# Hybrid decoder trunk: the second weight pair on ScalarE's queue, the first weight cast on VectorE, nine warming products

## The chip, the cores and the metric

The kernel runs on one core of one Trainium2 chip. The metric is the device time of one execution in microseconds. Three executions of the kernel before are shown, and a fourth was profiled.

## The reference, cut to what matters

The layer is a decoder block over 272 tokens (16 meta tokens and 256 others) of width 2048. It normalises the tokens, multiplies them by one wide input projection, runs eight retention heads and four mLSTM heads on slices of the product, projects back, and applies a gated MLP with a causal convolution.

```python
u = rmsnorm(h, norm_mix)
proj = u @ w_in.astype(u.dtype)
q_r, k_r, v_r, g_r, q_m, k_m, v_m, o_m, i_pre, f_pre = jnp.split(proj, IN_OFFSETS, axis=-1)
...
mix = jnp.concatenate([ret, hm], axis=-1).astype(h.dtype) @ w_out.astype(h.dtype)
h = h + mix
u = rmsnorm(h, norm_ffn)
up = causal_dwconv(u @ w_up.astype(u.dtype), ffn_conv_w, ffn_conv_b)
gate, val = jnp.split(up, [FFN_DIM], axis=-1)
return h + (jax.nn.silu(gate) * val) @ w_down.astype(h.dtype)
```

## The kernel before, in words

Every product runs on TensorE in float32r with both operands split into a high and a low part. For an operand pair (w, x) three matmuls are made: high by high, high by low, low by high. The high part of a weight (`whi`) is a cast of the loaded tile (`wraw`), and the low part (`wlo`) is `wraw` minus `whi`. The same holds for the activations: `xh` is the cast of the token matrix `hT` times the gain of the norm (ScalarE, L219), and `xl` is the rest (VectorE, L220).

The change touches the first stage alone, the loop at L207. It walks over 16 blocks of 128 rows of the inner dimension (k = 0 to 15): the first two blocks singly, then seven pairs (2,3), (4,5) to (14,15). For each step it loads the tokens `hT` (L209), in the first step also the 16 columns of `par` that hold the gain (L211), and the weights `wraw` from `in_w` (L215). The weights of one block are 320 columns wide: 256 columns of two projections (tiles `k_ps` and `q_ps`) and 64 of the gates. Then it makes `xh` and `xl` per block, `whi` (L224), `wlo` (L226) and the gates' low part (L227). Eight matmuls of a block follow: three for `k_ps` and three for `q_ps` (L136, L137, L139), and two for the gates (L235, L236).

SyncE's queue (SPq) issues nearly all transfers. The weights of blocks 0 and 1 are issued by ScalarE's queue (ACTq). `wraw` has four buffers, so the load of the fifth step waits until the first buffer is read. Ahead of the loop TensorE runs `WARM` products of a constant tile (L199), whose result is not used; one such product shows as two matmul records in the trace.

The order of the instructions on each engine is not the order of the program's text: a scheduler with a simulated time line chooses it when the kernel is built, unless a line asks for an order with `tc.issue_after`. In the text the activations (L219) stand ahead of the cast of the weights (L224).

Of the kernel before, what the change touches and what calls it, by code (L numbers as in the profile page):

```python
# [31 lines left out]
HALF = KT // 2  # L32
GW = 64
W0 = GW + 2 * P
WARM = 8

# [45 lines left out]
def trunk(ctx: ExitStack, tc: tile.TileContext, io, out: bass.AP):  # L84
    nc = tc.nc

    def pool(name, bufs, **kw):
        return tc.tile_pool(name=name, bufs=bufs, **kw)
# [12 lines left out]
    def pcol(name, i, n=1):  # L101
        a = _COLS[name][0]
        return par[:, a + i : a + i + n]
# [28 lines left out]
    def mmk(ps, w, ks, xh, xl, first, last):  # L132

        hi, lo = w
        for k, kk in ks:
            nc.tensor.matmul(ps, hi[:, k, :], xh(kk), start=kk == first, stop=False)  # L136
            nc.tensor.matmul(ps, hi[:, k, :], xl(kk), start=False, stop=False)  # L137
        for k, kk in ks:
            nc.tensor.matmul(ps, lo[:, k, :], xh(kk), start=False, stop=kk == last)  # L139
# [6 lines left out]
    def project(src, xh, xl, t0, ps=None):  # L146

        if ps is None:
            ps = mm.tile([P, 512], F32, name="mmps")
        for half in range(2):  # L150
            half_tile(ps[:, : xh.shape[2] - t0], src, half, xh, xl, t0)
        return ps
# [6 lines left out]
    def rsqrt_m2(work, v, n, after):  # L159

        r0 = work.tile([P, T], F32, name="r0", bufs=1)
        with tc.issue_after(table("natural_log_exp_and_others", after).ins):
            nc.scalar.activation(r0[:, :n], v, AF.Ln, bias=epsc)
        nc.scalar.activation(r0[:, :n], r0[:, :n], AF.Exp, scale=-0.5)
        t = work.tile([P, T], F32, name="rt", bufs=1)
        nc.scalar.activation(t[:, :n], r0[:, :n], AF.Square)
        nc.vector.scalar_tensor_tensor(out=t[:, :n], in0=v, scalar=EPS, in1=t[:, :n], op0=ALU.add, op1=ALU.mult)
        nc.vector.scalar_tensor_tensor(out=r0[:, :n], in0=t[:, :n], scalar=3.0, in1=r0[:, :n], op0=ALU.subtract, op1=ALU.mult)
        return r0
# [27 lines left out]
    warm = at.tile([P, 512], F32, name="atps")  # L197
    for _ in range(WARM):
        nc.tensor.matmul(warm[:, :P], ones, ones, start=True, stop=True)  # L199
# [6 lines left out]
    with pool("sq", 1, side="right") as sqp:  # L206
        for k0, k1 in [(0, 1), (1, 2)] + [(k, k + 2) for k in range(2, KT, 2)]:  # L207
            n = k1 - k0
            nc.sync.dma_start(hT[:, k0:k1, :], io["xT"][:, k0:k1, :])  # L209
            if k0 == 0:  # L210
                nc.sync.dma_start(par[:, 0:KT], io["par"][:, 0:KT])  # L211
            raw = wpool.tile([P, 2, W0], F32, name="wraw", bufs=4)[:, :n, :]

            queue = nc.scalar if k0 < 2 else nc.sync
            load = queue.dma_start(raw, io["w0"][:, k0:k1, :])  # L215
            if k0 >= 2:
                last_load = load
            for k in range(k0, k1):
                nc.scalar.activation(xh[:, k, :], hT[:, k, :], AF.Copy, scale=pcol("gmix", k))  # L219
                nc.vector.scalar_tensor_tensor(out=xl[:, k, :], in0=hT[:, k, :], scalar=pcol("gmix", k),  # L220
                                               in1=xh[:, k, :].bitcast(F32), op0=ALU.mult, op1=ALU.subtract)

            hi = wpool.tile([P, 2, W0 + GW], F32R, name="whi", bufs=5)[:, :n, :]
            copied = nc.scalar.copy(hi[:, :, 0:W0], raw)  # L224
            lo = wpool.tile([P, 2, 2 * P], F32R, name="wlo", bufs=5)[:, :n, :]
            nc.vector.tensor_tensor(out=lo, in0=raw[:, :, 0 : 2 * P], in1=hi[:, :, 0 : 2 * P].bitcast(F32), op=ALU.subtract)  # L226
            parted = nc.vector.tensor_tensor(out=hi[:, :, W0:], in0=raw[:, :, 2 * P :], in1=hi[:, :, 2 * P : W0].bitcast(F32), op=ALU.subtract)  # L227
            for k in range(k0, k1):
                i = k - k0
                first, last = k == 0, k == KT - 1  # L230
                for j, (ps, t0) in enumerate(((k_ps, 0), (q_ps, TQ))):
                    w = hi[:, :, j * P : (j + 1) * P], lo[:, :, j * P : (j + 1) * P]
                    mmk(ps[:, : T - t0], w, [(i, k)], lambda k: xh[:, k, t0:], lambda k: xl[:, k, t0:], 0, KT - 1)
                if not last:
                    nc.tensor.matmul(gates_ps[:, :T], hi[:, i, 2 * P :], xh[:, k, :], start=first, stop=False)  # L235
                nc.tensor.matmul(gates_ps[0:GW, :T], hi[:, i, 2 * P : W0], xl[:, k, :], start=False, stop=False)  # L236
                if last:
                    nc.tensor.matmul(gates_ps[:, :T], hi[:, i, 2 * P :], xh[:, k, :], start=False, stop=True)
        with tc.issue_after(last_load.ins):
            nc.sync.dma_start(par[:, KT:NPAR0], io["par"][:, KT:NPAR0])  # L240

        v0_ps = project(next(tiles), xh, xl, 0, at.tile([P, 512], F32, name="atps"))

        sum4 = None
        for k in range(0, KT, 4):

            sq = rope if k % 8 else sqp.tile([P, 4, T], F32, name="sq" if k else "sum4")
            with tc.issue_after(copied.ins):
                squared = nc.scalar.activation(sq, hT[:, k : k + 4, :], AF.Square)
            if k:  # L250
                with tc.issue_after(parted.ins), tc.high_priority():
                    nc.vector.tensor_tensor(out=sum4, in0=sum4, in1=sq, op=ALU.add)
            else:
                sum4 = sq
        with tc.high_priority():
            for n in (2, 1):
                nc.vector.tensor_tensor(out=sum4[:, 0:n, :], in0=sum4[:, 0:n, :], in1=sum4[:, n : 2 * n, :], op=ALU.add)
            ms = at.tile([P, 512], F32, name="atps")
            nc.tensor.matmul(ms[:, :T], inv_dm, sum4[:, 0, :], start=True, stop=True)
            r = rsqrt_m2(wk, ms[:, :T], T, squared)  # L260
            nc.vector.tensor_scalar(out=rstd1, in0=r[:, :T], scalar1=-0.5, scalar2=None, op0=ALU.mult)
# [39 lines left out]
    for i, x in enumerate((rM, rm)):  # L301
        hi, lo = parts[0:MH, i, :], parts[GW // 2 : GW // 2 + MH, i, :]
# [332 lines left out]
    for half in range(2):  # L635
        mh = midp.tile([P, NHF, SEQ], F32R, name="mh")
        ml = midp.tile([P, NHF, SEQ], F32R, name="ml")
        for jj in range(NHF):
# [10 lines left out]
            copied = nc.scalar.copy(mh[:, jj, :], gt)  # L649
# [147 lines left out]
```

## Time and the profile before

| | |
|---|---|
| median of three runs | 1236.26 us (1235.96 to 1236.76) |
| the profiled execution | 1236.06 us |
| its span, first to last instruction | 1234.3 us |
| outside the span | 1.76 us |
| granted TensorE clock, mean | 0.998 |

The profiled execution is 0.20 us under the median and inside the range of the three runs. The span runs from the first to the last instruction; the time of an execution has 1.76 us beside it.

### The profile page before, as it was taken

The page shows a single profiled execution, that of the slowest core. Times are in us where ns is not written, and L with a number is a line of the kernel's source. Part 1 is how long each engine was busy: PE and PEld are TensorE (multiplying, and loading weights), DVE is VectorE, ACT ScalarE, POOL GpSimd, SP SyncE. Part 2 cuts the span into 40 slices and gives each one's busy share as a digit, 9 for nine tenths or more (in the row PEclk, how much of TensorE's full clock was granted, in tenths as well). Part 3 has the DMA queues.
Part 4 walks back from the last instruction along what each step waited for, and adds up shares of the span by engine and source line. Part 5 has one row for each costly group of instructions (what it writes and reads, how often), then busy time and mean ns, then how long its engine had stood idle before and what let it go on. Part 6 is the DMA issues. An engine that isn't in the chain of part 4 may idle for free.

```text
span 1234.3 us, 22246 instructions
## 1 busy us (share of the span) xinstructions
PE 1223.8 (99%) x9082; PEld 1173.4 (95%) x9082; DVE 831.9 (67%) x1227; ACT 654.9 (53%) x879; POOL 63.0 (5%) x71
## 2 busy tenths in 40 slices
PE   9999999999999999999999999999999999999997
PEld 9999999999999999999999998889999999998886
DVE  8957777756665766778878764445677677664452
ACT  8756656555556556555555543334555555554441
POOL 0100011111110110000000000000000000000000
PEclk9999999999999999999999999999999999999999
DMA  8755454555553656555555655665555555555661
GB/s 276 265 172 164 151 164 160 170 169 163 175 178 121 221 177 217 185 177 186 186 176 187 187 179 187 189 189 186 185 184 181 182 185 184 179 185 187 187 205 69
DMA packets 63687, 224.30 MB, mean 182 GB/s; under 512 B 7392, under 2 KB 8544, under 8 KB 63456
## 3 DMA queue, kind: packets, MB, share of 16 engines
q1 hardware_dynamic: 62352, 219.26, 56.2%
q0 software_dynamic: 656, 2.76, 0.7%
q8 instruction: 71, 1.16, 0.4%
q10 hardware_dynamic: 576, 0.85, 0.2%
q14 instruction: 32, 0.26, 0.1%
HBM read 220.75 MB, written 2.10 MB: 181 GB/s over the span
## 4 chain that ended last, share of the span: by engine, by line
PE 98%; ACT 0%; DMA 0%; DVE 0%; issue 0%; SPq 0%; DVEq 0%; ACTq 0%
PE mmps L137 25%; PE mmps L136 25%; PE mmps L139 25%; PE atps L664 7%; PE atps L665 7%; PE atps L668 7%; PE atps L353 1%; PE atps L345 0%; PE atps L330 0%; DMA wraw<-in_w 0%; PE atps L136 0%; PE atps L139 0%; PE atps L354 0%; PE atps L137 0%; PE atps L346 0%; PE atps L355 0%
## 5 line engine op out<-in xcount | busy, mean ns | idle before, releaser
L127 ACT CAST whi<-wraw 128x1024 fp32r<-128x1024 f32 x404 | 422.9, 1049 | 473.5 <-PE mmps L137 256.8
L129 DVE TENSOR_TENSOR wlo<-wraw,whi 128x1024 fp32r<-128x1024 f32 x404 | 494.7, 1226 | 192.9 <-ACT whi L127 188.0
L137 PE MATMUL mmps<-ul,whi 128*128 128x258 f32 x1408 | 345.8, 283 | 0.0
L136 PE MATMUL mmps<-uh,whi 128*128 128x258 f32 x1408 | 345.5, 282 | 0.0
L136 PEld LDWEIGHTS mmps<-uh,whi 128*128 128x128 f32 x1408 | 266.1, 189 | 0.1
L137 PEld LDWEIGHTS mmps<-ul,whi 128*128 128x128 f32 x1408 | 265.1, 188 | 0.1
L137 PE MATMUL mmps<-xl,whi 128*128 128x272 f32 (+2 forms) x864 | 219.3, 287 | 0.0
L136 PE MATMUL mmps<-xh,whi 128*128 128x272 f32 (+2 forms) x864 | 219.2, 287 | 0.0
L139 PE MATMUL mmps<-uh,wlo 128*128 128x258 f32 x1408 | 198.9, 284 | 0.0
L139 PEld LDWEIGHTS mmps<-uh,wlo 128*128 128x128 f32 x1408 | 182.4, 189 | 0.0
L137 PEld LDWEIGHTS mmps<-xl,whi 128*128 128x128 f32 x864 | 162.9, 189 | 0.0
L136 PEld LDWEIGHTS mmps<-xh,whi 128*128 128x128 f32 x864 | 162.6, 188 | 0.0
L664 PE MATMUL atps<-whi,mh 128*128 128x512 f32 (+1 forms) x360 | 140.5, 391 | 0.0
L665 PE MATMUL atps<-whi,ml 128*128 128x512 f32 (+1 forms) x360 | 140.2, 390 | 0.0
L139 PE MATMUL mmps<-xh,wlo 128*128 128x272 f32 (+2 forms) x864 | 126.6, 285 | 0.0
L139 PEld LDWEIGHTS mmps<-xh,wlo 128*128 128x128 f32 x864 | 114.2, 188 | 0.0
L668 PE MATMUL atps<-wlo,mh 128*128 128x512 f32 (+1 forms) x360 | 110.8, 388 | 0.0
L578 DVE TENSOR_TENSOR cu<-mmps,rstd 128x258 f32<-128x258 f32 x88 | 37.6, 427 | 97.3 <-PE mmps L139 96.8
L664 PEld LDWEIGHTS atps<-whi,mh 128*128 128x128 f32 x360 | 67.6, 188 | 15.8
L668 PEld LDWEIGHTS atps<-wlo,mh 128*128 128x128 f32 x360 | 67.0, 188 | 16.0
L665 PEld LDWEIGHTS atps<-whi,ml 128*128 128x128 f32 x360 | 67.6, 188 | 15.1
L137 PE MATMUL mmps<-mixl,whi 128*128 128x258 f32 x256 | 63.1, 283 | 0.0
(211 smaller groups left out, 1049.4 us busy)
## 6 DMA issues: line engine op xcount, KB each, us to landing
wraw<-in_wu SPq DMA_DIRECT2D x176, 512.0 KB, 3.5
wraw<-in_wi SPq DMA_DIRECT2D x108, 512.0 KB, 3.6
wraw<-in_wd SPq DMA_DIRECT2D x88, 512.0 KB, 3.5
wraw<-in_wo SPq DMA_DIRECT2D x32, 512.0 KB, 3.7
wraw<-in_w SPq DMA_DIRECT2D x7, 320.0 KB, 5.5
hT<-in_xT SPq DMA_DIRECT2D x7, 272.0 KB, 5.9
e<-in_decay POOLq DMA_DIRECT2D x8, 209.0 KB, 3.4
gfin<-in_gfin POOLq DMA_DIRECT2D x1, 1024.0 KB, 6.1
```

The source lines that it names most:

```text
L127: nc.scalar.copy(hi, raw)
L129: nc.vector.tensor_tensor(out=lo, in0=raw, in1=hi.bitcast(F32), op=ALU.subtract)
L136: nc.tensor.matmul(ps, hi[:, k, :], xh(kk), start=kk == first, stop=False)
L137: nc.tensor.matmul(ps, hi[:, k, :], xl(kk), start=False, stop=False)
L139: nc.tensor.matmul(ps, lo[:, k, :], xh(kk), start=False, stop=kk == last)
L353: nc.tensor.matmul(ps[:, 0:NQ], lhs(0), pT[:, 0:CA], start=True, stop=False)
L578: nc.vector.tensor_tensor(out=u, in0=ps[:, :NQ], in1=rstd2, op=ALU.mult)
L664: nc.tensor.matmul(ps, mh[:, k, rows], hi[:, i, cols], start=k == 2 * first, stop=False)
L665: nc.tensor.matmul(ps, ml[:, k, rows], hi[:, i, cols], start=False, stop=False)
L668: nc.tensor.matmul(ps, mh[:, k, rows], lo[:, i, cols], start=False, stop=k == 2 * last + 1)
```

## The change

Three edits. The weights of the pair (2,3) are issued by ScalarE's queue, as a third transfer behind those of blocks 0 and 1, and no longer by SyncE's queue. The cast of block 0's weights is made by VectorE (`tensor_copy`), and no longer by ScalarE. And there is one more warming product, nine in place of eight.

```diff
-WARM = 8
+WARM = 9
...
-            queue = nc.scalar if k0 < 2 else nc.sync
+            queue = nc.scalar if k0 < 4 else nc.sync
             load = queue.dma_start(raw, io["w0"][:, k0:k1, :])
-            if k0 >= 2:
+            if k0 >= 4:
                 last_load = load
...
             hi = wpool.tile([P, 2, W0 + GW], F32R, name="whi", bufs=5)[:, :n, :]
-            copied = nc.scalar.copy(hi[:, :, 0:W0], raw)
+            if k0 == 0:
+
+                nc.vector.tensor_copy(hi[:, :, 0:W0], raw)
+            else:
+                copied = nc.scalar.copy(hi[:, :, 0:W0], raw)
```

## Rows read from the trace of the kernel before

**Rows 1.** The page, part 1: busy time, share of the span, instructions.
```profile
PE 1223.8 (99%) x9082; PEld 1173.4 (95%) x9082; DVE 831.9 (67%) x1227; ACT 654.9 (53%) x879; POOL 63.0 (5%) x71
```

**Rows 2.** The page, part 4: the chain that ended last, by engine.
```profile
PE 98%; ACT 0%; DMA 0%; DVE 0%; issue 0%; SPq 0%; DVEq 0%; ACTq 0%
```

**Rows 3.** That chain in its first 25 us, its longest piece: start, duration, what.
```profile
2.59 4.41 DMA wraw<-in_w
```

**Rows 4.** Timeline, TensorE around the pair (2,3): start, duration, what, idle before.
```profile
6.89 0.29 PE L236 MATMUL atps<-xl,whi 128*64 128x272 f32 x1
...
7.80 0.39 PE L136 MATMUL atps<-xh,whi 128*128 128x272 f32 x1 [0.62 <-ACT whi L224]
...
8.28 0.28 PE L137 MATMUL mmps<-xl,whi 128*128 128x262 f32 x1
8.53 0.39 PE L139 MATMUL atps<-xh,wlo 128*128 128x272 f32 x1
...
8.76 0.29 PE L139 MATMUL mmps<-xh,wlo 128*128 128x262 f32 x1
```

**Rows 5.** Timeline, ScalarE: its issues and its first instructions.
```profile
0.74 0.90 ACTq L215 DMA_DIRECT2D wraw<-in_w  x2
1.67 1.28 ACT L224 ACT_TABLE_LOAD   x1 [1.67 <-PEq L787]
3.79 0.46 ACT L224 CAST whi<-wraw 128x320 fp32r<-128x320 f32 x1 [0.84 <-DMA wraw<-in_w]
4.16 0.52 ACT L219 ACTIVATE xh<-hT,par 128x272 fp32r<-128x272 f32 x1
6.05 0.94 ACT L219 ACTIVATE xh<-hT,par 128x272 fp32r<-128x272 f32 x2 [0.60 <-DMA hT<-in_xT]
7.02 0.72 ACT L224 CAST whi<-wraw 128x640 fp32r<-128x640 f32 x1
```

**Rows 6.** Timeline, SyncE's queue ahead of the pair's weights.
```profile
1.65 0.90 SPq L209 DMA_DIRECT2D hT<-in_xT  x2
```

**Rows 7.** The tile par, its first load: us from issue (at 1.18) to landing.
```profile
DMA to landing us min/median/max: 2.9/2.9/2.9
```

**Rows 8.** Groups by line and form, VectorE: count, busy us, mean ns, idle before.
```profile
L220 DVE SCALAR_TENSOR_TENSOR xl<-hT,par,xh 128x272 fp32r<-128x272 f32 x16 | 7.3, 497 | 0.5 <-ACT xh L219 0.5
L226 DVE TENSOR_TENSOR wlo<-wraw,whi 128x512 fp32r<-128x512 f32 x7 | 4.8, 688 | 0.4 <-ACT whi L224 0.3
L226 DVE TENSOR_TENSOR wlo<-wraw,whi 128x256 fp32r<-128x256 f32 x2 | 0.8, 422 | 2.6 <-ACT whi L224 2.6
L261 DVE TENSOR_SCALAR rstd<-r 128x272 f32<-128x272 f32 x1 | 0.3, 303 | 0.0
```

**Rows 9.** Timeline, TensorE: warming records in short windows, and the first real matmul.
```profile
3.14 0.63 PE L199 MATMUL atps<-ones 128*128 128x128 f32 x2
...
3.57 0.63 PE L199 MATMUL atps<-ones 128*128 128x128 f32 x2
...
4.15 0.39 PE L199 MATMUL atps<-ones 128*128 128x128 f32 x2
...
4.26 0.28 PE L199 MATMUL atps<-ones 128*128 128x128 f32 x1
...
4.73 0.39 PE L136 MATMUL atps<-xh,whi 128*128 128x272 f32 x1 [0.19 <-ACT xh L219]
```

**Rows 10.** Timeline, the pair (6,7) on ScalarE, VectorE and TensorE.
```profile
9.68 0.94 ACT L219 ACTIVATE xh<-hT,par 128x272 fp32r<-128x272 f32 x2 [0.36 <-DMA hT<-in_xT]
...
11.27 0.69 DVE L226 TENSOR_TENSOR wlo<-wraw,whi 128x512 fp32r<-128x512 f32 x1
...
12.57 0.29 PE L139 MATMUL atps<-xh,wlo 128*128 128x272 f32 x1
```

**Rows 11.** Windows of 0.4 us: PE busy (count), granted clock, DMA share, GB/s.
```profile
3.40:3.80 0.40, 0.40 (x4) 1.00 1.08 387
4.20:4.60 0.40, 0.34 (x4) 1.00 0.77 114
```

## The prediction

> **What bounds the kernel now.** I read the page's engine line first: TensorE is busy 1223.8 of 1234.3 us [rows 1], and the chain that ended last is TensorE for 98% of the span [rows 2]. So a change can pay only in the 10.5 us in which TensorE does not work, and this one touches only its start. I then read the chain in its first 25 us. It does not start on TensorE: it runs through the transfer of the pair (2,3)'s weights, issued at 2.59 and landed 4.41 later at 7.00 [rows 3], then through ScalarE's cast of them at 7.02 [rows 5], and from 7.80 through TensorE's matmuls [rows 4]. What happens ahead of that is covered by it, unless it ends later than 7.80.
>
> The timeline tells how much stands there to be won. The last matmul of block 1 starts at 6.89 [rows 4], and matmuls that are not held up start some 0.12 apart, so the next could start at 7.01. It starts at 7.80: 0.79 lost. The fourth matmul of the pair starts at 8.28, three steps and 0.48 behind the first, against 0.36: 0.12 more for the slow step after a stall. Then the first low part is late: the L139 at 8.53 follows by 0.25, and the next at 8.76 by 0.23 [rows 4], against 0.12 twice, another 0.24. The whole is 0.79 + 0.12 + 0.24 = 1.15 us, 0.09% of the time. From 8.76 on TensorE is never idle in this stage. That is the ceiling of the change unless it makes a difference elsewhere.
>
> **The pair's weights on ScalarE's queue.** ScalarE's queue issues its two transfers from 0.74 to 1.64 [rows 5]; a third, at 0.45 each, stands at 1.65 to 2.10 in place of SyncE's 2.59 [rows 3], 0.94 earlier. Behind it on ScalarE stands the table load: 1.67 goes to about 2.12, and with 1.28 it ends at 3.40 instead of 2.95. ScalarE then waits for data until 3.79 [rows 5], so the issue costs nothing; it would cost only past 0.84 us. SyncE's queue loses one issue: the tokens of (4,5) and all behind them go out by up to one issue, 0.45, earlier, until the ring of four weight buffers holds them up.
>
> The landing does not follow by 0.94. The transfers share the DMA engines, which move 387 GB/s at 3.40:3.80 and only 114 GB/s at 4.20:4.60, with a share of 0.77 [rows 11]. That hole is what an earlier issue can fill: (387 - 114) x 0.4 us = 109 KB, and 109 KB at 387 GB/s is 0.28 us. So from 7.00 the last of the pair's two transfers comes to about 6.7 by the hole alone; the full 0.94 gives 6.06. Weights and tokens of the pair now come side by side, and the tokens, which ScalarE gets at 6.05 [rows 5], may be late in turn. I take the weights at 6.2 (between 6.06 and 6.7, nearer to the first, since they no longer queue behind the pair's tokens) and the tokens at 6.1 to 6.4.
>
> **Which comes first on ScalarE.** This decides the sum. Before, ScalarE takes blocks 2 and 3 of the activations at 6.05 for 0.94 us, to 6.99, and the cast at 7.02 [rows 5]. So the chain names the transfer, but ScalarE itself was free only at 6.99: if the order stays, weights that land earlier win no more than some 0.1. For block 0, whose weights come by ScalarE's queue, the cast at 3.79 stands ahead of the activation at 4.16 [rows 5], against the order of the text. I expect the same for the pair when its weights are issued ahead of its tokens. Then: cast from 6.2 to 6.92 (0.72), the first activation to 7.44 (0.52), the first matmul near 7.48 instead of 7.80 [rows 4, 5]. TensorE has two or three matmuls that need no more than these. VectorE must make the low part of block 2 (0.50) and those of the weights (0.69) [rows 8]; taken straight after the activation the first is there by 7.95, behind the weights' by about 8.25. Three matmuls, at 7.48, 7.71 and 7.83, then a short wait, and the sixth starts at 8.3 to 8.5, where it stood at 8.76 [rows 4]: 0.3 to 0.45, I take 0.4. By the same steps weights at 6.06 give 0.55, and at 6.7 the first matmul is at 7.98 and only the later wait of 0.24 is won back: 0.06. Tokens and weights both on time for 7.01 would give the ceiling of 1.15.
>
> **The cast of block 0 on VectorE.** Before, the cast (3.79) holds the activation to 4.16 [rows 5]. The gain's column lands at 1.18 + 2.9 = 4.08 [rows 7], so the activation moves by 0.08 at most, to about 4.1. No copy of this form is in the trace. From below, a tensor_scalar over 272 columns took 0.303; from above, the two-operand form took 0.422 for 256 columns and 0.688 for 512, 1.04 ns a column, hence 0.49 for 320 [rows 8]. A single-operand copy is nearer to the first: I take 0.35, done at 4.14; the upper bound gives 4.28. Either is ahead of the activation's end at 4.62, which TensorE also needs. The first real matmul goes from 4.73 [rows 9] to about 4.67, or not at all. And it is hidden: whatever block 0 wins, TensorE still waits for the pair. Its price if that wait is gone is these 0.06 us. I count 0.
>
> **The ninth warming product.** Two warming records lie between 3.14 and 3.57, 0.21 apart; the last two start at 4.15 and 4.26, 0.11 apart [rows 9]. So the spacing halves in between, though the granted clock is put down as 1.00, that is 2.4 GHz, on both sides [rows 11]. Two more records at 0.11 end their issue at 4.26 + 3 x 0.11 = 4.59, ahead of the first real matmul. At 0.21 each they would end it near 4.8 and move it by 0.1, which the pair's wait covers as well. I count 0, with -0.1 to +0.1.
>
> **What limits the gain behind it.** If TensorE is earlier by g from 8.76 on, the pair (6,7) must be ready by that much earlier. Its tokens hold ScalarE up at 9.68, and its weights' low part is made at 11.27 to 11.96, while TensorE takes it at 12.57 [rows 10]: 0.61 of slack. So where that pair's tokens don't land earlier, no more than about 0.6 is kept, and the ceiling of 1.15 needs earlier tokens there too. A gain of 0.4 passes.
>
> **The sum.** 1236.06 (profiled) - 0.4 + 0 + 0 = 1235.66. The profiled execution stands 0.20 under the median of three, so a median may stand as much above; I say 1235.7.
>
> **The rivals.**
> *The order changes nothing on arrival.* Two queues share the same engines, and the pair's two transfers together end where they ended, 6.9 to 7.0, or ScalarE keeps the activations first and the cast starts at 6.9 to 7.05. TensorE then starts the pair at 7.68 to 7.83: -0.1 to 0, 1236.0 to 1236.1. For it speaks that ScalarE was free only at 6.99; against it, the hole of 109 KB and the order seen for block 0. Chance 0.28.
> The Trainium skill (DMA: Bandwidth & Descriptors, Issuing engines are not separate DMA queues) says that transfers issued from several engines interleave on the same 16 DMA engines and that several issuers save only the time to issue; the trace's 387 GB/s next to 114 GB/s lets neither be excluded.
>
> *The pair's tokens become late (the other side).* The weights' packets now take DMA time while the pair's tokens move. With activations first, each 0.1 that they land past 6.05 is 0.1 on the cast, and it turns to a loss from 6.15 on. At the worst they land at 7.00: activations 7.02 to 7.96, cast at 7.9 to 8.62, TensorE at 8.65 instead of 7.80, 0.85 lost, 1236.9. Against it: SyncE's queue issues these tokens where it did, from 2.12 [rows 6]. Chance 0.15.
>
> *The order shifts far behind the start.* A simulated time line orders every engine; other arrivals in it can put other instructions first in later stages. No row shows it, and TensorE's 10.5 idle us are a bound on what it can win. The price of one ScalarE table load in the wrong place is 1.28 [rows 5]: one to three of those either way, 1232 to 1240. Chance 0.12, a little over half of it for slower.
>
> **How the numbers follow.** The forecast has 0.45: 1235.7, its own range 1235.0 to 1236.2. To leave no more than 2 in 10 out, the range takes in the first rival, most of the second and the spread of a median of three (before: -0.3 to +0.5): 1234.6 to 1237.0. About what a measurement of this kernel can tell from no change is 0.2%, 2.5 us: 1233.8 to 1238.7. The forecast and the first two rivals lie inside it with all their bounds; only the third reaches out. Same 0.92, faster 0.03, slower 0.05.
>
> **What will show it.** The chain's first pieces: the weights' transfer should start near 1.65 and land near 6.2, with the cast ahead of the activations of blocks 2 and 3, and the wait of L136 for L224 should fall from 0.62 to about 0.3. If the cast stands behind them near 7.0, the first rival holds; if the idle time ahead of those activations grows past 0.60, the second; if order or idle time changes behind 25 us, the third. The forecast would be wrong by more than its range if TensorE's slow spacing came back after the warming, or if the first two blocks' tokens became late.

## The result, and the profile after

The changed kernel takes 1238.83 us (median of 12 executions, 1238.21 to 1239.97), the kernel before in the same comparison 1236.32 (1235.96 to 1236.76). The ratio is 1.0022, 95% interval 1.0013 to 1.0031: 2.5 us slower, with an interval clear of 1, and just above the 1238.7 up to which the prediction called a time the same. The forecast of 1235.7 and its range up to 1237.0 were wrong, and on the other side.

The profiled execution after took 1238.94 us with a span of 1237.1, 2.8 longer than before. The text is longer by four lines, so L224 is now L226 (the cast on VectorE) and L228 (on ScalarE), L226 is L230, L236 is L240, L238 is L242, L252 is L256, L279 is L283; lines up to L220 keep their numbers. The page's engine line after:

```profile
PE 1224.7 (99%) x9084; PEld 1174.0 (95%) x9084; DVE 832.4 (67%) x1228; ACT 652.8 (53%) x877; POOL 62.9 (5%) x71
```

TensorE is busy 0.9 us longer than in [rows 1], and the span grew by 2.8: so 1.9 us of new idle time are to be found. TensorE's waits after (engine, tile, line, waited for; us in total, times, longest):

```profile
PE atps L139 <- DVE wlo L129: 1.7, 1, 1.7
PE atps L199 <- DVE ones L107: 1.1, 1, 1.1
PE atps L136 <- ACT xh L219: 1.0, 1, 1.0
PE atps L349 <- ACT floor L466: 0.2, 1, 0.2
```

The 0.6 for the pair's weights is gone from this list, as the change meant it to be. But two waits stand there that before were not or were small: 1.0 for the very first activation (0.19 in [rows 9]), and 1.7 for a low part of weights at L129, which lies behind the first stage. ScalarE's timeline shows the first:

```profile
0.74 1.38 ACTq L215 DMA_DIRECT2D wraw<-in_w  x3
4.08 1.28 ACT L219 ACT_TABLE_LOAD   x1 [4.08 <-DMA par<-in_par]
5.37 0.52 ACT L219 ACTIVATE xh<-hT,par 128x272 fp32r<-128x272 f32 x1
5.80 0.44 ACT L228 CAST whi<-wraw 128x320 fp32r<-128x320 f32 x1
6.78 0.52 ACT L219 ACTIVATE xh<-hT,par 128x272 fp32r<-128x272 f32 x1 [0.54 <-DMA hT<-in_xT]
7.21 0.71 ACT L228 CAST whi<-wraw 128x640 fp32r<-128x640 f32 x1
```

The table load, which ran at 1.67 while ScalarE had nothing to do [rows 5], now starts at 4.08, released by the gain's column: exactly the landing in [rows 7]. ScalarE's three issues end at 2.12, so the engine stands idle for 1.96 us with the load in front of it. The first activation ends at 5.89 instead of some 4.68. The second block's activation then waits 0.54 for its tokens, which landed 5.1 us after their issue at 1.65, at 6.75. TensorE, at the first matmul of block 0, of block 1 and of the pair, at the last matmul of the stage, and at the eight products behind it:

```profile
5.94 0.39 PE L136 MATMUL atps<-xh,whi 128*128 128x272 f32 x1 [0.98 <-ACT xh L219]
...
7.36 0.39 PE L136 MATMUL atps<-xh,whi 128*128 128x272 f32 x1
...
8.62 0.29 PE L136 MATMUL atps<-xh,whi 128*128 128x272 f32 x1
...
22.76 0.29 PE L242 MATMUL atps<-xh,whi 128*128 128x272 f32 x1
...
26.80 1.27 PE L139 MATMUL atps<-xh,wlo 128*128 128x272 f32 x8 [1.74 <-DVE wlo L129]
```

The same two late places in the kernel before:

```profile
21.85 0.29 PE L238 MATMUL atps<-xh,whi 128*128 128x272 f32 x1
...
23.98 1.16 PE L139 MATMUL atps<-xh,wlo 128*128 128x272 f32 x8
```

So the loss is 5.94 - 4.73 = 1.21 at the first matmul, 8.62 - 7.80 = 0.82 at the pair (the pair's own stall is no longer there), 22.76 - 21.85 = 0.91 at the end of the stage, and 26.80 - 23.98 = 2.82 at the eight products. That last figure is the whole growth of the span. The start accounts for 0.91 of it, and 1.91 arise between 22.8 and 26.8, where the diff touches nothing. VectorE's timeline there, after:

```profile
19.54 1.29 DVE L256 TENSOR_TENSOR sum<-sum,rope 128x1088 f32<-128x1088 f32 x1
23.09 0.43 DVE L283 COPY g<-atps 4x272 f32<-4x272 f32 x1 [2.26 <-PE atps L242]
23.45 1.27 DVE L256 TENSOR_TENSOR sum<-sum,sq 128x1088 f32<-128x1088 f32 x1
24.73 0.43 DVE L284 TENSOR_TENSOR g<-atps,g 4x272 f32<-4x272 f32 x1
25.18 0.43 DVE L283 COPY qT<-atps 4x272 f32<-4x272 f32 x1
25.54 2.34 DVE L129 TENSOR_TENSOR wlo<-wraw,whi 128x1024 fp32r<-128x1024 f32 x2
```

and before:

```profile
19.52 1.29 DVE L252 TENSOR_TENSOR sum<-sum,rope 128x1088 f32<-128x1088 f32 x1 [0.69 <-ACT rope L249]
20.92 1.29 DVE L252 TENSOR_TENSOR sum<-sum,sq 128x1088 f32<-128x1088 f32 x1
22.18 0.43 DVE L279 COPY g<-atps 4x272 f32<-4x272 f32 x1
22.53 2.34 DVE L129 TENSOR_TENSOR wlo<-wraw,whi 128x1024 fp32r<-128x1024 f32 x2
24.90 0.43 DVE L280 TENSOR_TENSOR g<-atps,g 4x272 f32<-4x272 f32 x1
```

The third sum of squares (the one with `sq`) and the copy of the gates have changed places. The copy needs the stage's last matmul, which comes at 22.76; in front of the sum it holds VectorE idle for 2.26 us, and the sum then falls behind it. Two more short steps of the gates, which before came behind the low part (24.90), now stand ahead of it as well (24.73 and 25.18). So the low part that TensorE needs starts 2.45 behind the copy instead of 0.35, at 25.54 instead of 22.53. No instruction was moved there by hand: the scheduler, with other arrivals at the start, chose another order.

### The profile page after: what moved, and what is told of

It reads as the page before. It is cut to its first block, busy times and chain, and to the rows that moved or that the text cites. A ratio compares the mean times of both kernels' runs of the same rounds, so it can differ in the third digit from the quotient of the medians.

```text
span 1237.1 us, 22248 instructions
## 1 busy us (share of the span) xinstructions
PE 1224.7 (99%) x9084; PEld 1174.0 (95%) x9084; DVE 832.4 (67%) x1228; ACT 652.8 (53%) x877; POOL 62.9 (5%) x71
## 3 DMA queue, kind: packets, MB, share of 16 engines
q10 hardware_dynamic: 720, 1.18, 0.3%
## 4 chain that ended last, share of the span: by engine, by line
PE 98%; ACT 1%; DVE 0%; issue 0%; DMA 0%; DVEq 0%; SPq 0%; ACTq 0%
PE mmps L137 25%; PE mmps L136 25%; PE mmps L139 25%; PE atps L668 7%; PE atps L669 7%; PE atps L672 7%; PE atps L357 1%; PE atps L349 0%; PE atps L334 0%; PE atps L139 0%; PE atps L358 0%; PE atps L137 0%; PE atps L136 0%; PE atps L350 0%; DMA par<-in_par 0%
## 5 line engine op out<-in xcount | busy, mean ns | idle before, releaser
L129 DVE TENSOR_TENSOR wlo<-wraw,whi 128x1024 fp32r<-128x1024 f32 x404 | 494.6, 1226 | 192.6 <-ACT whi L127 187.5
```

Of the source, the lines that this page charges most:

```text
L129: nc.vector.tensor_tensor(out=lo, in0=raw, in1=hi.bitcast(F32), op=ALU.subtract)
```

## The experiments

Each kernel was timed next to the kernel before, whose medians in the three groups were 1236.33, 1236.42 and 1236.32. The first three take the change apart, the next ones repair one suspected cause after the other, and the last control the repairs. Each kernel has one profile, taken of one of its executions.

### One part at a time

The queue edit alone:

```
-            queue = nc.scalar if k0 < 2 else nc.sync
+            queue = nc.scalar if k0 < 4 else nc.sync
...
-            if k0 >= 2:
+            if k0 >= 4:
```

> The queue edit alone: ScalarE's queue issues the pair's weights, the cast of block 0 stays on ScalarE, eight warming products. Theory A (the queue edit carries all three lateness: the table load that waits for the gain's column, block 1's tokens landing near 6.7 instead of 4.55, and VectorE's gates copy ahead of its sum, so that TensorE waits 1.7 us for a low part near 25 us): 1238.5 to 1239.3, as the whole change. Theory B (the loss needs VectorE's cast, since only that takes the cast away from in front of the table load): within 0.4 of before, 1236.0 to 1236.7. Theory C (the ninth product costs the time): as B.

1239.58 us (1238.54 to 1240.28), ratio 1.0024 [1.0014, 1.0035]: the whole loss and no less, 0.3 above the upper end of what was expected. Its eight executions overlap with the changed kernel's. Its waits of TensorE and ScalarE's table load:

```profile
PE atps L139 <- DVE wlo L129: 1.7, 1, 1.7
...
PE atps L136 <- ACT whi L224: 1.5, 1, 1.5
```

```profile
4.09 1.28 ACT L219 ACT_TABLE_LOAD   x1 [4.09 <-DMA par<-in_par]
```

Both late places are there although the cast of block 0 is still ScalarE's. With the longer queue the scheduler puts the activation ahead of that cast by itself, and the table load goes with it. So I had the cause of the late load half wrong: not the removal of the cast alone, but anything that makes an activation ScalarE's first computation.

The cast alone:

```
-            copied = nc.scalar.copy(hi[:, :, 0:W0], raw)
+            if k0 == 0:
+                nc.vector.tensor_copy(hi[:, :, 0:W0], raw)
+            else:
+                copied = nc.scalar.copy(hi[:, :, 0:W0], raw)
```

> VectorE's cast of block 0 alone, all else as before. Theory A: the table load stands ahead of the first activation and waits with it, near 4.08 to 5.37, and the first real matmul starts near 5.9 instead of 4.73; but the pair's weights still land at 7.0, so most of it is covered: the pair starts at 8.1 to 8.3 instead of 7.80 and the later wait for the low part shrinks, 0.1 to 0.5 lost, 1236.4 to 1236.8; VectorE's order near 20 us is that of before, and no wait stands at 25 us. Theory B (the table load is the main cost): 1.2 lost, 1237.5.

1237.56 us (1236.46 to 1237.96), ratio 1.0006 [0.9997, 1.0015]. The table load starts at 4.09 here too, and TensorE waits 1.1 us for the first activation, but the wait at L129 is missing. So the order near 20 us comes with the queue edit, the late table load with either edit. Its executions fall into two groups, 4 from 1236.46 to 1236.58 and 7 from 1237.27 to 1237.96; the upper group, to which the profiled one belongs, shows this (TensorE, start and duration):

```profile
4.20 0.64 PE L199 MATMUL atps<-ones 128*128 128x128 f32 x2
...
4.42 0.42 PE L199 MATMUL atps<-ones 128*128 128x128 f32 x1
...
5.96 0.59 PE L136 MATMUL atps<-xh,whi 128*128 128x272 f32 x1 [1.12 <-ACT xh L219]
6.35 0.42 PE L136 MATMUL mmps<-xh,whi 128*128 128x262 f32 x1
6.57 0.43 PE L239 MATMUL atps<-xh,whi 128*128 128x272 f32 x1
...
9.93 0.43 PE L137 MATMUL atps<-xl,whi 128*128 128x272 f32 x1
10.15 0.37 PE L136 MATMUL mmps<-xh,whi 128*128 128x262 f32 x1
10.36 0.28 PE L137 MATMUL mmps<-xl,whi 128*128 128x262 f32 x1
10.48 0.29 PE L139 MATMUL atps<-xh,wlo 128*128 128x272 f32 x1
```

Behind the idle 1.12 us the matmuls start 0.22 apart up to 10.15, then 0.12 apart. The wide spacing was there ahead of the idle time too: the last warming records, at 4.20 and 4.42, are still 0.22 apart. The changed kernel's profile has 0.12 from 6.17 on, but for short waits, and its warming products had come to the narrow spacing before they ended:

```profile
4.58 0.39 PE L199 MATMUL atps<-ones 128*128 128x128 f32 x2
...
4.69 0.28 PE L199 MATMUL atps<-ones 128*128 128x128 f32 x1
```

So the median of 1237.56, which stands at the figure of theory B, is not shown to be the plain price of the late start: the lower group lies within theory A's 1236.4 to 1236.8. No execution of the lower group was profiled.

The ninth product alone (`WARM = 9`):

> The ninth warming product alone. Theory A: hidden, 1236.1 to 1236.5, first real matmul at 4.73 to 4.85. Theory C (warming costs): 0.2 to 0.4 more, 1236.5 to 1236.7.

1236.31 us (1235.95 to 1237.11), ratio 1.0001 [0.9992, 1.0010]: nothing, as counted. Its first real matmul starts at 4.91, later than the expected 4.73 to 4.85, since all its warming records stay 0.21 apart to the last at 4.84; the pair's wait covers that (7.79 against 7.80).

### The changed kernel with VectorE's order put back

```
-                    nc.vector.tensor_tensor(out=sum4, in0=sum4, in1=sq, op=ALU.add)
+                    added = nc.vector.tensor_tensor(out=sum4, in0=sum4, in1=sq, op=ALU.add)
+                if k == 8:
+                    summed = added
...
-        nc.vector.tensor_copy(o, gates_ps[g : g + MH, :T])
+        with tc.issue_after(summed.ins):
+            nc.vector.tensor_copy(o, gates_ps[g : g + MH, :T])
```

> The whole change, and the copy of the gates is asked to stand behind the third square's sum on VectorE, as it stood before. Theory A: the wait of TensorE for the low part near 25 us (1.74) is gone and with it 1.9 us, while the start stays late by 1.0: 1236.7 to 1237.3. Rival (the order there only shows the late start, and the wait moves on): no more than 0.3 won, 1238.5.

1237.73 us (1236.33 to 1237.97), 0.4 above what was expected: its highest execution is below the changed kernel's lowest, 1238.21, and the wait at L129 is gone. Its times too fall into two groups, 4 from 1236.3 to 1236.9 and 7 from 1237.5 to 1238.0. The lower group of the changed kernel is 1238.2 to 1238.9, so like against like (1238.59 against 1236.66, the middles of the two lower groups) the order costs some 1.9, as the 1.91 of the traces. In its profile, one of the upper group, the warming records stay 0.21 apart to the last at 4.85, the first matmul starts at 5.99 behind an idle 0.72, and the next ones come 0.22 apart.

The same with `WARM = 12`, so that TensorE does not stand idle ahead of the late first matmul:

> The whole change with the copy of the gates behind the sum, and twelve warming products in place of nine, which keep TensorE busy through the late table load. Theory A (runs near 1237.8 in the run without them are those whose first matmuls go at half speed, behind TensorE's idle time from about 5 to 6): all runs at 1236.4 to 1236.9, matmul spacing 0.12 from the first. Rival (the two groups of times come from elsewhere): median 1237.7 again, both groups.

1236.92 us (1236.43 to 1237.46), in one group: the first matmul is as late as before (6.04), the spacing is 0.12, and the eight products start at 24.93. That is the cost of the late start alone: 24.93 - 23.98 = 0.95 in the traces, 0.5 in the medians, whose ratio of 1.0005 [0.9996, 1.0013] does not tell it from nothing. The wide spacing that goes on behind the idle time is thereby a cost of its own, some 1.2 us in the executions that have it (1237.84 against 1236.66, the middles of the two groups of the kernel with VectorE's order put back). Three more products both fill the idle time and give the spacing time to fall, which it does at about 5.3 in this profile; the two were not separated.

### A table load that waits for nothing

A copy of one constant column, issued behind ScalarE's transfers, should take the table load with it and away from the gain. At first it was written into a small tile of its own, in the changed kernel, in the changed kernel with VectorE's order put back, and (at `k0 == 1`) in the cast-only kernel:

```
+    tiny = consts.tile([P, 1], F32, name="tiny")
...
+            if k0 == 2:
+                with tc.issue_after(load.ins), tc.high_priority():
+                    nc.scalar.copy(tiny, epsc)
```

> The whole change, and a one-column copy on ScalarE behind its three issues, so that the table load waits for no transfer. Theory A (block 1's tokens, late behind the pair's weights, hold TensorE up anyway, and VectorE's order near 20 us still costs 1.9): first real matmul at 4.7 to 5.0, a wait for the tokens of block 1 near 6.2 to 7.3, 1238.2 to 1238.7, with the slow matmul spacing at the start gone and so the runs closer together. Theory B (the table load is the cost of the start): 1.2 less than the change, 1237.3 to 1237.7.

> As the run with the table load first, and the copy of the gates behind the sum. Theory A: 1.9 less than that run, 1236.3 to 1236.8, within 0.5 of before; what is left is the late tokens of block 1. Rival (moving the pair's weights pays once the two accidents are gone): 0.4 under before, 1235.7 to 1236.0.

> Without the queue edit: VectorE's cast and nine warming products, and the one-column copy that frees the table load. Theory A: the cast alone, its accident removed, is hidden by the pair's weights: 1236.1 to 1236.5, first real matmul at 4.65 to 4.9, the pair at 7.75 to 7.85. Rival (the cast itself loads VectorE too much): 1236.6 or more.

1241.83 (1240.17 to 1242.66), 1238.66 (1238.15 to 1239.28) and 1238.42 us (1237.96 to 1239.14): each above what was expected. The table load did start early in them, at 2.15, 2.15 and 1.66. What went wrong lay far behind: between 500 and 600 us TensorE has 830 matmul records in each of the three, 834 in the kernel before, always busy and at the same granted clock. The suspect was the tile of 4 bytes a partition, which may move what is placed behind it; no run shows the addresses. So the next group wrote the copy into a column of a tile that exists and is filled only later, `nc.scalar.copy(rstd1[:, 0:1], epsc)`, and one kernel gave the kernel before nothing but a spare tile:

```
+    spare = consts.tile([P, 1], F32, name="spare")
+    nc.gpsimd.memset(spare, 0.0)
```

> The kernel before with one spare tile of one column (4 bytes a partition) among its constants, written once by GpSimd and read by nothing. Theory A (what slowed the earlier runs is where the later tiles lie): 1238.2 to 1238.9, all of it as slower matmuls between 480 and 1100 us, 830 matmul records in 500 to 600 us and not 834. Rival (it was the copy on ScalarE): 1236.3.

1238.32 us (1237.95 to 1239.60), ratio 1.0015 [1.0006, 1.0024], as expected. A tile that nobody reads costs 2.0 us. Windows of this kernel (us, TensorE busy and count, granted clock, DMA share, GB/s):

```profile
500.00:600.00 100.00, 100.00 (x830) 1.00 0.61 182
```

and of the kernel before:

```profile
500.00:600.00 100.00, 100.00 (x834) 1.00 0.60 184
```

So the three misses say nothing against the table load. The repeats without the tile, first the changed kernel:

> The whole change with the table load first, as before, but the one-column copy writes a column of a tile that is there already, so that no tile moves. Theory A (the new tile of the earlier runs slowed the matmuls of the gated MLP by 2.3 us; block 1's tokens and VectorE's order are what is left): 1238.2 to 1239.2. Rival (the table load is the cost of the start, 1.2): 1237.3 to 1237.7.

1239.79 us (1237.97 to 1240.16), above what was expected. The first matmul is at 4.92 instead of 5.94, so the table load is repaired, but VectorE's order is as in the changed kernel and the wait of 1.74 at L129 is still there, and the profiled execution pays for it a second time. Windows of TensorE, same columns:

```profile
25.00:26.00 1.00, 0.00 (x0) 1.00 0.00 0
...
27.00:28.00 1.00, 1.00 (x8) 0.71 0.86 98
28.00:29.00 1.00, 1.00 (x6) 0.50 0.85 344
29.00:30.00 1.00, 1.00 (x7) 0.50 0.97 369
30.00:31.00 1.00, 1.00 (x7) 0.59 0.53 217
31.00:32.00 1.00, 1.00 (x11) 1.00 0.06 25
```

After standing still TensorE is granted 0.50, its 1.2 GHz level, for some 3 us, and does 6 to 7 matmuls a microsecond where the changed kernel's profile has 10 at 1.00. Five executions lie from 1237.97 to 1238.66, six from 1239.79 to 1240.16. The stretch from the eight products to the next eight takes 4.64 us in this profile and 3.12 in the changed kernel's: these 1.5 us are most of the 1.8 between the middles of the two groups.

The changed kernel with both repairs, the early table load and VectorE's order:

> The whole change with the table load first and the gates' copy behind the sum, no new tile. Theory A: 1236.2 to 1236.8, that is 1.9 under the run with the table load first alone, and not under before, since block 1's tokens are late behind the pair's weights. Rival (the queue edit pays once both accidents are gone): 1235.7 to 1236.0.

1236.55 us (1236.16 to 1236.79), ratio 1.0001 [0.9992, 1.0009], its highest below the lowest 1237.97 of the kernel without the second repair. ScalarE's start in it:

```profile
2.15 1.28 ACT L218 ACT_TABLE_LOAD   x1 [2.15 <-issue]
3.44 0.19 ACT L218 COPY rstd<-epsc 128x1 f32<-128x1 f32 x1
4.05 0.52 ACT L222 ACTIVATE xh<-hT,par 128x272 fp32r<-128x272 f32 x1 [0.42 <-DMA par<-in_par]
4.48 0.44 ACT L231 CAST whi<-wraw 128x320 fp32r<-128x320 f32 x1
6.46 0.52 ACT L222 ACTIVATE xh<-hT,par 128x272 fp32r<-128x272 f32 x1 [1.54 <-DMA hT<-in_xT]
```

The load starts at 2.15 behind the third issue, as the prediction had it. What remains is the last line: ScalarE idle for 1.54 us until the second block's tokens, and TensorE waits 0.8 for their activation. The eight products start at 24.58, still 0.60 behind the kernel before. One profile cannot price that: the kernels with the ninth product alone, with the spare tile and with the cast and the early load, none of which has the queue edit, start them at 24.12, 24.64 and 24.68.

The cast alone with the early table load:

> Without the queue edit, VectorE's cast, nine products, the table load first, no new tile. Theory A: 1236.0 to 1236.5, level with before. Rival (the 2 us of the earlier run came from the cast or the copy and not from the new tile): 1238.4 again.

1236.48 us (1236.05 to 1237.04), ratio 0.9999 [0.9990, 1.0007], against 1237.56 without it (and without the ninth product). Here TensorE still waits 0.6 for the pair's weights, so whatever block 0 wins is covered, as the prediction said of it. The three kernels with the small tile stand 2.04, 2.11 and 1.94 above these three repeats without it, which is the spare tile's price again.

No version beat the kernel before by more than the measurement can tell.

## Why the prediction was wrong, point by point

*What bounds the kernel now.* The reading of the start was right, its 1.15 us the right sum of its rows, and the argument from it too narrow: "touches only its start" holds for the diff, not for the orders that the scheduler makes from it.

*The pair's weights on ScalarE's queue: the step that failed first.* I wrote that behind the issue "stands the table load: 1.67 goes to about 2.12, and with 1.28 it ends at 3.40". I asked what stands ahead of the load, not what the load waits for. In [rows 5] it belongs to the cast; with an activation first, it starts at the gain's landing. Shown by the changed kernel (4.08), by each edit alone (4.09), and by the early copy, which brings it to 2.15 and the first matmul to 4.92. By the traces it costs 1.21 us at the first matmul and 0.91 at the end of the stage, where the forecast had 0.4 won. That the load holds one of the two waits of the activation behind it, for `hT` and for `par`, is read from the row's releaser; how the program assigns that wait was not tried.

*The same part, the landing.* "I take the weights at 6.2" was wrong for this profile: issued at 1.66, they landed 5.3 later, at 6.95, against 7.00. The first rival had this. But its "6.9 to 7.0" is one pair of profiles: in the eight profiles with the queue edit these weights landed between some 6.3 and 7.2, in the six without it between 7.0 and 8.1, with middles of some 6.7 and 7.4. So the earlier issue did bring them forward in the middle of the profiles, by some 0.7 of its 0.94 us, and some five of the eight lie between the prediction's 6.06 and 6.7. That rival's sentence on the Trainium skill ("DMA: Bandwidth & Descriptors", "Issuing engines are not separate DMA queues") has the transfers of several queues interleave on the same engines, and the trace agrees: what follows shows other transfers later. The hole in [rows 11] was indeed filled, and to no avail (window after, columns as there):

```profile
4.20:4.60 0.40, 0.40 (x4) 1.00 0.90 338
```

But other transfers landed later. Block 1's tokens landed 5.1 us after issue instead of 2.9, the pair's tokens 5.4 instead of 3.9. In the kernels with the queue edit block 1's tokens took 3.6 to 5.1 and the pair's 4.9 to 5.5, in those without it 2.9 to 4.0 and 3.9 to 4.7.

*Which comes first on ScalarE.* Right: the pair's cast stands at 7.21 ahead of the activations of blocks 2 and 3 (7.83), and TensorE's 0.62 for it is gone. But the order won nothing, since both the activations and the weights were later than I had put them.

*The cast of block 0 on VectorE.* Its price was right: 0.33 us measured where I took 0.35, hidden. "The first real matmul goes from 4.73 to about 4.67, or not at all" failed, by the table load: 5.94. With the load early it could not be seen either: in the kernels with nine products and an early load the first matmul starts at 4.92, right behind the last warming record.

*The ninth warming product.* Its price was right: nothing (1.0001). Its working was not: "two more records at 0.11" holds in the changed kernel's profile, while in that of the ninth product alone all records stay 0.21 apart and the first matmul comes 0.18 later, which the pair's wait covers. And "if TensorE's slow spacing came back after the warming", given as a sign of being wrong, is near to what the upper groups of times show: there it had not gone.

*The rivals.* "The pair's tokens become late" named the right mechanism one block too far on: it was block 1's tokens, for which TensorE waits once all else is repaired; their price, at most some 0.6 by the traces and 0.2 by the medians, is not told from nothing. "The order shifts far behind the start", at a chance of 0.12, made the larger part of the loss; the forecast's 0.5 under the kernel before failed without it, since with the order put back the median stays 1.4 above, and 0.5 above with twelve products. Its place was VectorE near 20 us, and its price 1.91, not a table load's 1.28. Both repairs together bring the median back to 0.23 us over the kernel before (0.6 by the traces), so the late load and the order are shown to make most of the 2.5 between them. In the medians the order repaired takes 1.10 and the early load then 1.18; like against like the order is 1.9, and the late load some 0.1 to 0.4 plus the 1.2 of the wide spacing in the executions that have it. Had the table load been read right, the sum would have been 1236.06 + 0.91, about 1237, inside "same" and still short of the 1238.83; the 1.91 could not be had from the rows, only a larger chance for that rival.

## What to carry to other kernels

Before an instruction at the head of an engine is moved away, ask what the next one waits for and what stands in front of it: a table load takes the place of the first computation, waits included, and a first computation on a resident constant keeps it early. An earlier issue on another queue need not be an equally earlier landing where the DMA engines are shared, and other transfers may pay for it; list the small ones that land in the same microseconds, and who waits for them, and read a landing from more than one profile. Where a scheduler makes the orders, compare each engine's order over the whole kernel with the one before ahead of trusting any sum worked out for the edited place.

## What the runs showed of the hardware that was not expected

TensorE that stood still for 1.74 us near 25 us sometimes resumes at half its rate for some 3 us: 6 to 7 matmuls a microsecond at a granted clock of 0.50, in the profile of the changed kernel with the early table load and no small tile. Three other profiles have the same 1.74 us and resume at 1.00 (the changed kernel, the queue edit alone, the first kernel with the small tile). What decides which execution is spared stays open.

At the start it is another matter. The spacing of the matmuls falls from some 0.22 to 0.12 at a moment that differs from profile to profile, and there may be no idle time ahead of it: at about 4.2 us in the kernel before, 4.5 in the changed kernel, and only past 6.4 in that kernel with the early table load, whose matmuls follow the warming products at once:

```profile
6.19 0.42 PE L137 MATMUL mmps<-xl,whi 128*128 128x262 f32 x1
6.41 0.42 PE L139 MATMUL mmps<-xh,wlo 128*128 128x262 f32 x1
```

In the three profiles in which it had not fallen when TensorE ran out of work (the queue edit, the cast, and the change with VectorE's order put back) the wide spacing lasted to 10.2 to 10.4. That fits the two groups of times at the start, one profile a kernel. What sets the moment stays open. The granted clock is put down as 1.00 all the same: the windows of the cast-only kernel show (same columns)

```profile
7.00:8.00 1.00, 1.00 (x6) 1.00 0.93 328
```

so in this stretch it is the count, not the clock column, that tells.

A spare tile of 4 bytes a partition costs 2.0 us of 1236 (830 records in place of 834 in 100 us of matmuls that never wait). Four kernels with such a tile show 830; the ten profiles without it show 833 or 834. Part of the spare tile's loss may be its later start (TensorE waits 1.2 us instead of 0.6 for the pair's weights in its profile). That later tiles move is argued from the program, and why it slows the matmuls was not tried.
